# An encoder layer on one core: queries cast ahead of the fourth exponential, and the row tile, the norms and the residual additions in other places

## The chip, the cores and the metric

The kernel runs on one core of a Trainium2 chip. Its engines are TensorE (PE, whose weight loads are listed apart as PEld), VectorE (DVE), ScalarE (ACT), GpSimd (POOL) and SyncE (SP), which here only issues DMAs. Each engine works through its own instructions in order; semaphores hold an instruction until its inputs are there and its output's place is free. The metric is the time of one execution on the device, in microseconds. Before the change it was 1484.23 us, the median of three runs (1482.45 to 1485.06).

## The reference

One layer of a bidirectional encoder, applied to two sequences of 512 tokens with the same weights, all in float32:

```
def encoder_layer(x, ...):                       # x (1, 512, 1024)
    h = rms_norm(x, ln1)
    q, k, v, u, g_att, g_ssm = split(h @ w_in)   # 16 query heads and 4 key heads of 64
    q, k = rms_norm(q per head, q_gain), rms_norm(k per head, k_gain)
    y_att = windowed_attention(q, k, v, sink, bias, mask)   # blocks of 128, 3 key blocks each
    y_ssm = s5_branch(u, ...)                    # y * sigmoid(y @ w_glu + b_glu)
    mixed = sigmoid(g_att) * y_att + sigmoid(g_ssm) * y_ssm
    x = x + mixed @ w_out
    h2 = rms_norm(x, ln2)
    return x + square(relu(h2 @ w_up)) @ w_down  # 1024 -> 4096 -> 1024
```

## The kernel before

Both sequences go through the layer together, 1024 tokens, in tiles of 128 rows (partitions). Every large product is done in three matmuls: an operand in float32 is split into a rounded part `hi`, cast by ACT, and the rest `lo`, subtracted by DVE, and PE adds up hi·hi, hi·lo and lo·hi (L115 to L117, and with other names L724, L753, L1177). So in front of nearly every matmul stand an ACT cast and a DVE subtraction. The order of the instructions of an engine follows the order in which the program gives them, but a scheduler may move them within limits, and the tiles of a pool decide which bytes of memory a tile gets, and with it for whom it must wait.

**Attention** runs in eight steps, one for each pair of a sequence and a key head, each of four units (a block of 128 queries with its four heads). In a unit `cur` is the unit whose scores are being made and `prev` the unit before it, whose probabilities are turned and multiplied by the values. `cur.scores(h)` is PE (L1048, into a bank of PSUM called `sps`), `cur.largest(h)` is DVE (L1052: adds the bias and finds the maximum `nmx`), `cur.exp(h)` is ACT (L1058). `prev.turn(j)` transposes on PE (L1064), `prev.high(j)` casts on ACT (`ph`, L1068), `prev.low(j)` subtracts on DVE (L1073), `prev.value(j, s)` multiplies on PE (L1080). `rows` is the set of queries for a block that comes later: `norm` (L1012), `turn` (PE, L1018), `high` (the cast `qa` on ACT, L1023) and `low` (its rest on DVE, L1027). Between these stand the projections for later steps on PE (`project`, L724), whose weights are loaded by SP (L717), cast by ACT (`w_hi`, L718) and subtracted by DVE. In the last step the products of the state-space branch take that place (L1177, with the operand `act` from ACT L1162 and DVE L1170). At the end of a step `Divide` makes the reciprocals of the sums of the probabilities: it turns them (L1106), copies them into the tile `row` (L1108, 16x128), stores them by DMA (L1109), loads them again spread out as `fac` (L1114) and multiplies on POOL (L1119).

**The gated mix** follows (L1490 to L1528): products with w_glu on PE (L753) whose weights are split by ACT (`c_hi`, L736) and DVE (`c_lo`, L737), and on DVE the gates, the mix of both branches and the split of the mixed rows `at` (L1516 to L1528), which are then multiplied by w_out. The tile pool `ap` holds the attention's tiles, the pool `wyp` those of the scan and of weights.

**The output projection and the second norm** (L1330 to L1680): the tokens of the second sequence go in three passes, t = 1 to 3. In each, `old.norm()` is the DVE operation L1439 (its factor `rs` comes from POOL, L1434), `old.turn()` the transposes of the result on PE (L1447), and `old.old_rows(0, 1)` two subtractions on DVE of rows of the first sequence (L1462).

**The MLP** is done with seven products in place of eight (Strassen and Winograd): the four quarters of the operands are first added to or subtracted from each other. In the down projection `product_d(n)` (L1907) makes product n in groups of two row pairs r = 0, 2, 4 and so on: the piece of the left operand `d_a` and of the weights `k1`, `k2`, `k3` are loaded, combined on DVE (L1923), and both are split, with casts on ACT (L1928) and subtractions on DVE (`a_lo`, `b_lo`, L1929). Then come 24 matmuls into four banks. The results are added up in the tiles q1, q3, q4, q5 (128x2048 each), to which the residual `xq`, loaded from memory, is added by one DVE operation each: L1948 ahead of product 5, L1955 ahead of product 6 and L1970 ahead of product 2.

Of the kernel before, what the change touches and what calls it, by code (L numbers as in the profile page):

```python
# [11 lines left out]
F32 = mybir.dt.float32  # L12
# [6 lines left out]
P = 128  # L19
# [10 lines left out]
G = 4  # L30
HD = 64
BLOCK = 128
NB = SEQ // BLOCK
# [30 lines left out]
def hybrid_layer(ctx, tc, x, xT, rel, onehot, early, w_qkv, w_ug, q_gain, k_gain, sink,  # L64
                 b_re, b_im, c_re, c_im, d_skip, w_glu, b_glu, w_out, ln2, w_up, w_down, out):
    nc = tc.nc
    V, S, PE, GP, SP = nc.vector, nc.scalar, nc.tensor, nc.gpsimd, nc.sync
# [203 lines left out]
    with tc.tile_pool(name="xin", bufs=2, reuse_waits="tile") as xin, tc.tile_pool(name="ssmc", bufs=1) as sc:  # L271
# [10 lines left out]
        rows, columns, first_w = {}, {}, []  # L282
# [670 lines left out]
    with tc.tile_pool(name="att", bufs=2, reuse_waits="tile") as ap:  # L953
# [138 lines left out]
        class Divide:  # L1092
# [10 lines left out]
            def turn(self):  # L1103
                j, sq = self.j, self.sq
                pt = tps()
                PE.transpose(pt[0:G * NB, 0:P], self.rs, ident)  # L1106
                row = ap.tile([G * NB, P], F32, tag="row", name="row", bufs=1)
                S.copy(row, pt[0:G * NB, 0:P])  # L1108
                self.queue.dma_start(rs_scr[sq, j * G:(j + 1) * G, :].rearrange("h (b t) -> (h b) t", b=NB), row)  # L1109
                self.fac = (ap.tile([P, 2, HALF], F32, tag="ya", name="fac") if self.last  # L1110
                            else evp.tile([P, 2, HALF], F32, tag="ev", name="fac"))
                for e in range(2):
                    src = rs_scr[sq, j * G + e, :]
                    self.queue.dma_start(self.fac[e * 64:(e + 1) * 64],  # L1114
                                         bass.AP(rs_scr.tensor, src.offset, [[0, 64], [2 * HALF, 2], [1, HALF]]))
# [83 lines left out]
        if True:  # L1199
            rows = entry()  # L1200
            for i, (j, sq) in enumerate(steps):
# [8 lines left out]
                for qb in range(NB):  # L1210
# [72 lines left out]
                        div.turn()  # L1283
                    if n3:
                        prev.value(1, 0)
                    cur.exp(3)
                    if n3 > 2:
                        prev.low(2)
                    if rows:
                        rows.high()  # L1290
                        rows.low()
                    project(4)
                    if i == len(steps) - 1:
# [295 lines left out]
    with tc.tile_pool(name="wout", bufs=1, reuse_waits="tile") as wb:  # L1589
        w_last = [wb.tile([P, KT, HALF], F32R, name=f"w{i}_23") for i in range(2)]  # L1590
        w4 += [[q[:, k:k + 4, :] for q in w_last] for k in (0, 4)]
        rows0 += [Rows(0, t) for t in range(2, 4)]
        ln2_bc = rn2.tile([P, D], F32, name="ln2_bc", bufs=1)
        SP.dma_start(ln2_bc, ln2.to_broadcast([P, D]))

        def pieces(n):
            for _ in range(n):
                nxt = raws[-1][0] + 1
                split_piece()
                if nxt < 2 * KT:  # L1600
                    load_piece(nxt)

        for k in (0, 4):
            for t in range(2):
                rows0[t].part(0, k, k + 4)
                if k:
                    rows0[t].end(0)()
                    pieces(1)
        for t in range(2, 4):
            for k in (0, 4):  # L1610
                rows0[t].part(0, k, k + 4)
                if k:
                    rows0[t].end(0)()
                pieces(1)
        for t in range(2):
            rows0[t].part(1, 0, 4)
            pieces(1)
        for t in range(4):
            if t < 2:
                rows0[t].part(1, 4, KT)  # L1620
                rows0[t].end(1)()
            else:
                rows0[t].half(1)()
            if t:
                rows0[t - 1].norm()
            if t > 1:
                rows0[t - 2].turn()
                rows0[t - 2].first_rows()
        rows1 = [Rows(1, 0)]
        add = rows1[0].half(0)  # L1630
        rows0[2].turn()
        rows0[2].first_rows()
        rows0[3].norm()
        t4 = slot_b.tile([P, KT, HALF], F32R, tag="act0", name="t4")
        T4 = [t4[:, 0:4, :], t4[:, 4:8, :]]
        add()
        add = rows1[0].half(1)
        rows0[3].turn()
        rows0[3].first_rows()
        for t in range(1, 4):  # L1640
            old = rows1[t - 1]
            rows1.append(Rows(1, t))
            nxt_add = rows1[t].half(0)
            add()
            if t > 1:
                rows1[t - 2].sums_b()
                rows1[t - 2].sums_c()
            old.old_rows(0, 1)
            old.norm()
            old.turn()  # L1650
            add = rows1[t].half(1)
            if t == 3:
                raws0 = [wb0.tile([P, 4, P], F32, tag="w_raw", name="u_raw0", bufs=2) for _ in range(2)]
                for i, raw in enumerate(raws0):
                    SP.dma_start(raw, w_up[0, :, i])
                up_raws = {0: slot_b.tile([P, 4, 4, P], F32, tag="b0", name="u_raw"),
                           1: slot_b.tile([P, 4, 4, P], F32, tag="b1", name="u_raw")}
                for r, raw in up_raws.items():
                    for i in range(2):
                        SP.dma_start(raw[:, i * 2:i * 2 + 2], w_up[r, :, i * 2:i * 2 + 2])  # L1660
                homes = [wb0.tile([P, 4, 4, P], F32R, tag=f"w{i}", name=f"f_{i}") for i in range(2)]
            nxt_add()
            if t == 3:
                first = [[(homes[r][:, 2 * i], homes[r][:, 2 * i + 1]) for i in range(2)] for r in range(2)]
                for raw, home in zip(raws0, first[0]):
                    first_parts(raw, home)()
            old.sums_a()
# [125 lines left out]
    def bank():  # L1793
        return ps_m.tile([P, HALF], F32, tag="bank", name="bank")
# [103 lines left out]
    with tc.tile_pool(name="down0", bufs=2, side="right", reuse_waits="tile") as d0, \  # L1898
# [5 lines left out]
        k2, k3 = [[dc.tile([P, 2, HALF], F32, name=f"k{i}_{r}") for r in range(NPAIR // 2)] for i in (2, 3)]  # L1904
        q1, q3, q4, q5 = [dc.tile([P, 4, HALF], F32, name=f"q{i}") for i in (1, 3, 4, 5)]

        def product_d(n):  # L1907

            ps = entry_ps if n == 1 else [bank() for _ in range(4)]
            for r in range(0, NPAIR, 2):  # L1910
                rs = slice(r, r + 2)
# [13 lines left out]
                for src, tag in ((a, "a"), (b, "b")):  # L1925
                    hi = (d0 if tag == "a" else dp).tile([P, 2, HALF], F32R, tag=tag + "_hi", name=tag + "_hi")
                    lo = dp.tile([P, 2, HALF], F32R, tag=tag + "_lo", name=tag + "_lo")
                    S.copy(hi, src)  # L1928
                    V.tensor_sub(lo, src, hi.bitcast(F32))  # L1929
                    hl.append((hi, lo))  # L1930
                pair_products(ps, hl, r)
            return ps

# [5 lines left out]
        def store(src, t, sq, c):  # L1939
            row = sq * HALF + t * P  # L1940
            SP.dma_start(out[row:row + P, c * HALF:(c + 1) * HALF], src)

        ps = product_d(1)
        SP.dma_start(k1[0], w_down[0, 0, :, 0:2, :])
        for t in range(4):
            S.copy(q1[:, t], ps[t])
        xq = residual(0, 0)
        V.tensor_add(q3, q1, xq)  # L1948
        xq = residual(0, 1)
        ps = product_d(5)  # L1950
        for t in range(4):
            S.copy(q5[:, t], ps[t])
            V.tensor_add(q4[:, t], q5[:, t], xq[:, t])
        xq = residual(1, 1)
        V.tensor_add(q5, q5, xq)  # L1955
        ps = product_d(6)
        for t in range(4):
            V.tensor_add(q1[:, t], ps[t], q1[:, t])
            V.tensor_add(q4[:, t], q1[:, t], q4[:, t])
# [6 lines left out]
        for t in range(4):  # L1966
            V.tensor_add(q1[:, t], ps[t], q1[:, t])
            V.tensor_add(q5[:, t], q5[:, t], q1[:, t])
            store(q5[:, t], t, 1, 1)
        V.tensor_add(q1, q1, xq)  # L1970
        ps = product_d(2)
        for t in range(4):
            V.tensor_add(q3[:, t], ps[t], q3[:, t])
            store(q3[:, t], t, 0, 0)
# [78 lines left out]
```

## Time and profile before

| | |
|---|---|
| median of three runs | 1484.23 us |
| the profiled execution | 1483.69 us |
| its span, from the first to the last instruction | 1481.9 us |
| mean granted clock of PE | 0.997 |
| instructions | 21572 |
| DMA | 243.86 MB in 129238 packets |

The profile is that of one execution. In its rows the first number is the start in us from the begin of the span, the second the busy time in us, then engine, line, operation, output, inputs and shape; x2 says that the row stands for two such instructions in a run. In brackets stands how long the engine had been idle and what ended it. A row with SPq is the issue of a DMA on SP. In the list of waits a row says who waited for which tile, by whom it was released, and the waiting time in all, how many times, and the mean.

### The profile page before, as it was taken

The numbers are of one execution on the slowest core, as the hardware profiler recorded it, in microseconds if no ns is written. First come the engines' busy times: TensorE is split into PE (matmuls) and PEld (weight loads), VectorE is DVE, ScalarE is ACT, GpSimd is POOL, SyncE is SP. The second block draws the span as 40 slices with busy tenths as digits, with TensorE's granted clock in tenths as the row PEclk, the third lists the DMA queues.
The fourth block names the chain that finished last, engine by engine and source line by source line (L and its number), as shares of the span: only waits on it lengthen the run. The fifth ranks groups of instructions, "written<-read, shape, count | busy, mean of one in ns | idle before, by whom it ended". The sixth has DMA issues, their size and how long they took to land.

```text
span 1481.9 us, 21572 instructions
## 1 busy us (share of the span) xinstructions
PE 1454.6 (98%) x7782; PEld 1235.8 (83%) x7782; DVE 1093.8 (74%) x1827; ACT 764.2 (52%) x1366; POOL 168.2 (11%) x270
## 2 busy tenths in 40 slices
PE   7999999999999999999999999999999999999998
PEld 5888888888998888987788888888888878888787
DVE  7799979964636888888973688877776588575553
ACT  5589862224426777787432355555545443333332
POOL 4111120000312333343100000000000000000000
PEclk9999999999999999999999999999999999999999
DMA  8355567359841313236864135544443894454441
GB/s 301 107 174 176 166 208 252 119 177 290 282 121 51 106 51 87 88 129 200 285 221 147 71 113 172 167 146 156 157 156 121 300 340 148 156 175 152 128 128 58
DMA packets 129238, 243.86 MB, mean 165 GB/s; under 512 B 16059, under 2 KB 59323, under 8 KB 129132
## 3 DMA queue, kind: packets, MB, share of 16 engines
q1 hardware_dynamic: 104684, 186.87, 40.1%
q10 hardware_dynamic: 21888, 46.15, 8.3%
q0 software_dynamic: 2560, 9.48, 2.0%
q8 instruction: 61, 1.00, 0.3%
q14 instruction: 45, 0.37, 0.1%
HBM read 173.20 MB, written 81.82 MB: 172 GB/s over the span
## 4 chain that ended last, share of the span: by engine, by line
PE 87%; DVE 5%; issue 3%; ACT 2%; DMA 2%; POOL 1%; SPq 0%; DVEq 0%; ACTq 0%; POOLq 0%
PE bank L116 13%; PE bank L117 13%; PE bank L115 13%; PE acc L141 11%; PE acc L724 7%; PE acc L753 4%; PE acc L115 3%; PE acc L117 3%; PE acc L116 3%; PE sps L604 2%; PE po L1080 2%; PE sps L860 2%; PE sps L1048 2%; PE tps L1064 2%; PE lag L619 1%
## 5 line engine op out<-in xcount | busy, mean ns | idle before, releaser
L116 PE MATMUL bank<-b_lo,a_hi 128*128 128x512 f32 x440 | 171.4, 390 | 2.4 <-DVE b_lo L1929 2.4
L117 PE MATMUL bank<-b_hi,a_lo 128*128 128x512 f32 x440 | 171.2, 389 | 0.0
L115 PE MATMUL bank<-b_hi,a_hi 128*128 128x512 f32 x440 | 170.5, 389 | 0.0
L724 PE MATMUL acc<-w_hi,hT 128*128 128x256 f32 x768 | 165.0, 292 | 0.0
L141 PE MATMUL acc<-hT,c_hi 128*128 128x512 f32 x512 | 161.1, 394 | 0.0
L1928 ACT CAST a_hi<-d_a 128x1024 fp32r<-128x1024 f32 x55 | 57.8, 1051 | 181.5 <-PE bank L116 178.5
L1929 DVE TENSOR_TENSOR a_lo<-d_a,a_hi 128x1024 fp32r<-128x1024 f32 x55 | 67.4, 1225 | 102.0 <-ACT a_hi L1928 99.9
L724 PEld LDWEIGHTS acc<-w_hi,hT 128*128 128x128 f32 x768 | 126.7, 190 | 1.7
L141 PEld LDWEIGHTS acc<-hT,c_hi 128*128 128x128 f32 x512 | 94.6, 188 | 21.1 <-issue 2.5
L724 PE MATMUL acc<-w_lo,hT 128*128 128x256 f32 x384 | 108.2, 282 | 0.0
L141 PE MATMUL acc<-hT,c_lo 128*128 128x512 f32 x256 | 100.2, 392 | 0.0
L117 PE MATMUL bank<-act,u_lo 128*128 128x512 f32 x256 | 99.6, 389 | 0.0
L115 PE MATMUL bank<-act,u_hi 128*128 128x512 f32 x256 | 99.6, 389 | 0.0
L116 PE MATMUL bank<-act,u_hi 128*128 128x512 f32 x256 | 99.6, 389 | 0.0
L116 PEld LDWEIGHTS bank<-b_lo,a_hi 128*128 128x128 f32 x440 | 82.6, 188 | 20.3 <-DVE b_lo L1929 3.2
L115 PEld LDWEIGHTS bank<-b_hi,a_hi 128*128 128x128 f32 x440 | 82.6, 188 | 17.3
L117 PEld LDWEIGHTS bank<-b_hi,a_lo 128*128 128x128 f32 x440 | 82.6, 188 | 17.1
L1058 ACT ACTIVATE p<-p,nmx 128x257 f32<-128x257 f32 (+1 forms) x128 | 72.2, 564 | 35.4 <-DVE nmx L1052 34.8
L724 PEld LDWEIGHTS acc<-w_lo,hT 128*128 128x128 f32 x384 | 73.0, 190 | 2.5
L1052 DVE CUSTOM_DVE_ANT_0 p<-sps,bias,nsink 128x256 f32<-128x256 f32 (+1 forms) x128 | 69.3, 542 | 2.9 <-PE sps L1048 0.4
L1713 ACT CAST u_hi<-s 128x512 fp32r<-128x512 f32 x64 | 39.3, 621 | 59.8 <-PE bank L116 36.9
L1929 DVE TENSOR_TENSOR b_lo<-k,b_hi 128x1024 fp32r<-128x1024 f32 x55 | 67.1, 1220 | 0.0
(389 smaller groups left out, 3627.8 us busy)
## 6 DMA issues: line engine op xcount, KB each, us to landing
d_a<-a_scr SPq DMA_DIRECT2D x55, 512.0 KB, 3.6
u_raw<-in_w_up_dram SPq DMA_DIRECT2D x32, 512.0 KB, 5.9
a_scr<-t ACTq DMA_DIRECT2D x64, 256.0 KB, 2.1
k<-in_w_down_dram SPq DMA_DIRECT2D x32, 512.0 KB, 5.7
a_scr<-a ACTq DMA_DIRECT2D x48, 256.0 KB, 3.3
c_raw<-in_w_ug_dram SPq DMA_DIRECT2D x44, 256.0 KB, 3.5
ct_scr<-ctab SPq DMA_DIRECT2D x16, 576.0 KB, 3.3
ctab_in<-ct_scr SPq DMA_DIRECT2D x32, 288.0 KB, 4.9
```

Of the source, the lines that this page charges most:

```text
L115: PE.matmul(ps, a[0], b[0], start=first, stop=False)
L116: PE.matmul(ps, a[0], b[1], start=False, stop=False)
L117: PE.matmul(ps, a[1], b[0], start=False, stop=last)
L141: PE.matmul(self.ps[s], self.w[p == 2][:, k, :], hT[s][p == 1][:, k, :], start=i % (3 * KT) == 0, stop=i % (3 * KT) == 3 * KT - 1)
L604: PE.matmul(ps[:, i * P:(i + 1) * P], bm[:, ri, g, :], u_sb[:, g, :], start=True, stop=True)
L724: PE.matmul(ps, act[p == 2][:, k, col:col + P], self.w[k // 4][p == 1][:, k % 4, :], start=i == 0, stop=i == 3 * KT - 1)
L753: PE.matmul(self.ps[s], w_g[self.m][p == 2][:, k, :], y_part(s, int(p == 1), k), start=k + p == 0, stop=k == KT - 1 and p == 2)
L1052: V.tensor_tensor_reduce(self.p[:, h, 1:1 + self.nk], self.s[h][:, 0:self.nk], biases[self.j][h][:, b0:b0 + self.nk], -1.0, nsink[:, hh:hh ...
L1058: S.activation(p, p, AF.Exp, bias=self.nmx[:, h:h + 1], scale=-1.0, accum_out=self.sums[:, h, self.qb:self.qb + 1])
L1713: S.copy(hi, src)
L1928: S.copy(hi, src)
L1929: V.tensor_sub(lo, src, hi.bitcast(F32))
```

## The change

It has four parts.

1. In the units whose `prev` has two key blocks and in which no keys are copied, the cast of the queries (`rows.high()`) is given ahead of `cur.exp(3)` instead of behind it. There is one such unit in each of the eight steps.
2. The tile `row` comes from the pool `wyp` instead of `ap`.
3. `old.norm()` is given ahead of `old.old_rows(0, 1)`.
4. Three of the additions of `xq` (128x2048) are made in four parts of 128x512 each and handed to `product_d`, which gives one of them in each group from the second on.

```
-                row = ap.tile([G * NB, P], F32, tag="row", name="row", bufs=1)
+                row = wyp.tile([G * NB, P], F32, tag="row", name="row", bufs=1)
...
+                    sooner = rows and n3 == 2 and not kd
+                    if sooner:
+                        rows.high()
                     cur.exp(3)
                     if n3 > 2:
                         prev.low(2)
                     if rows:
-                        rows.high()
+                        if not sooner:
+                            rows.high()
                         rows.low()
...
+            old.norm()
             old.old_rows(0, 1)
-            old.norm()
             old.turn()
...
-        def product_d(n):
-
+        def product_d(n, aside=()):
+
+            aside = list(aside)
...
+                if r and aside:
+                    aside.pop(0)()
                 pair_products(ps, hl, r)
...
+        def added(dst, src, xq):
+            return [lambda t=t: V.tensor_add(dst[:, t], src[:, t], xq[:, t]) for t in range(4)]
...
-        V.tensor_add(q3, q1, xq)
+        ps = product_d(5, added(q3, q1, xq))
         xq = residual(0, 1)
-        ps = product_d(5)
...
-        V.tensor_add(q5, q5, xq)
-        ps = product_d(6)
+        ps = product_d(6, added(q5, q5, xq))
...
-        V.tensor_add(q1, q1, xq)
-        ps = product_d(2)
+        ps = product_d(2, added(q1, q1, xq))
```

On ACT, in the unit of step 1 that makes the scores of its second block, the order is now the following (the difference; L1058 are exponentials, L1108 the copy into `row`, L1023 the cast of the queries, L1001 the squares for the norm of the next ones, L1084 a copy of the values' result):

```order
 L1058 ACTIVATE p,sm<-p,nmx 128x385
 L1108 COPY row<-tps 16x128
-L1058 ACTIVATE p,sm<-p,nmx 128x385
-L1023 ACTIVATE qa<-acc,gain_q 128x4x128
+L1023 ACTIVATE qa<-acc,gain_q 128x4x128
+L1058 ACTIVATE p,sm<-p,nmx 128x385
 L1001 ACTIVATE sq<-acc 128x256
 L1084 COPY ol<-po 64x512
```

The cast has changed places with the fourth exponential, and nothing else has moved there; on DVE `rows.low()` stands where it stood.

On SP, at the same place of step 1 (L717 are loads of weights for the projections, L1109 is the store of `row`, L1214 a copy within memory for the scan):

```order
 L717 DMA w_raw_5242<-in_w_qkv_dram 128x512
 L1214 DMA y2_scr_84<-y_scr_83 16x64x128
+L1109 DMA rs_scr_93<-row_5328 16x128
 L717 DMA w_raw_5349<-in_w_qkv_dram 128x512
-L1109 DMA rs_scr_93<-row_5328 16x128
 L717 DMA w_raw_5680<-in_w_qkv_dram 128x512
 L1214 DMA y2_scr_84<-y_scr_83 16x64x128
```

The store of `row` has moved ahead of one load of weights.

On DVE, at the start of product 5 in the down projection, the order before was (L1923 combines pieces of weights, L1929 splits, L1948 is the addition of the residual):

```order
L1929 TENSOR_TENSOR b_lo_12612<-k1_0_12316,b_hi_12611 128x1024
L1923 TENSOR_TENSOR k2_0_12324<-k3_0_12332,k2_0_12324 128x1024
L1923 TENSOR_TENSOR k1_0_12316<-k3_0_12332,k1_0_12316 128x1024
L1923 TENSOR_TENSOR k2_1_12325<-k3_1_12333,k2_1_12325 128x1024
L1929 TENSOR_TENSOR a_lo_12644<-d_a_12639,a_hi_12643 128x1024
L1948 TENSOR_TENSOR q3_12341<-q1_12340,xq_12594 128x2048
L1929 TENSOR_TENSOR b_lo_12648<-k1_1_12317,b_hi_12647 128x1024
L1923 TENSOR_TENSOR k2_2_12326<-k3_2_12334,k2_2_12326 128x1024
```

and it is now (the lines L1923, L1929 and L1948 of before are L1928, L1934 and L1951 here):

```order
L1934 TENSOR_TENSOR b_lo_12609<-k1_0_12316,b_hi_12608 128x1024
L1928 TENSOR_TENSOR k2_0_12324<-k3_0_12332,k2_0_12324 128x1024
L1951 TENSOR_TENSOR q3_12341<-q1_12340,xq_12594 128x512 x3
L1928 TENSOR_TENSOR k1_0_12316<-k3_0_12332,k1_0_12316 128x1024
L1934 TENSOR_TENSOR a_lo_12641<-d_a_12636,a_hi_12640 128x1024
L1934 TENSOR_TENSOR b_lo_12645<-k1_1_12317,b_hi_12644 128x1024
L1951 TENSOR_TENSOR q3_12341<-q1_12340,xq_12594 128x512
L1928 TENSOR_TENSOR k1_1_12317<-k3_1_12333,k1_1_12317 128x1024
L1928 TENSOR_TENSOR k2_1_12325<-k3_1_12333,k2_1_12325 128x1024
```

Three of the four quarters stand ahead of the second `b_lo`, the fourth behind it, and one combination of weights (`k2_1`) has moved behind it as well.

## The prediction

> **What bounds the kernel.** I read the page first, then what TensorE (PE) waited for, then each of those places in order of time.
>
> ```profile
> PE 1454.6 (98%) x7782; PEld 1235.8 (83%) x7782; DVE 1093.8 (74%) x1827; ACT 764.2 (52%) x1366; POOL 168.2 (11%) x270
> PE 87%; DVE 5%; issue 3%; ACT 2%; DMA 2%; POOL 1%; SPq 0%; DVEq 0%; ACTq 0%; POOLq 0%
> ```
> PE works 1454.6 of the 1481.9 us of the span, and the chain of work that ended last runs on PE for 87% of it. No other engine is near its limit, so only two things make this kernel shorter: fewer or shorter matmuls, or fewer waits of PE. The change leaves PE's instructions as they are (their order differs in two groups of matmuls only). What it can gain lies within the 27 us in which PE does nothing, and the four kinds of wait that its parts aim at are these (waiting us, times, mean us):
>
> ```profile
> PE sps L1048 <- DVE nmx L1052: 3.3, 7, 0.5
> PE bank L116 <- DVE b_lo L1929: 2.4, 2, 1.2
> PE acc L753 <- DVE c_lo L737: 2.0, 1, 2.0
> PE tps L1447 <- DVE rn_xn L1439: 0.8, 2, 0.4
> ```
> Together 8.5 us, with 12 waits. A wait costs more than its idle time, since the matmul behind it starts in an empty pipeline: below I take the loss from start to start, against the spacing of the same matmuls elsewhere.
>
> **Queries ahead of the fourth exponential.** Step 1, between the blocks 1 and 2 (us from the span's start, busy us, then idle before):
>
> ```profile
> 494.14 0.62 ACT L1058 ACTIVATE p<-p,nmx 128x385 f32<-128x385 f32 x1 [0.74 <-DVE nmx L1052]
> 494.76 0.67 ACT L1023 ACTIVATE qa<-acc,gain_q 128x512 fp32r<-128x512 f32 x1
> 494.90 0.60 PE L1064 MATMUL tps<-ident,p 128*128 128x128 f32 x4
> 495.46 0.76 DVE L1027 SCALAR_TENSOR_TENSOR qa<-acc,gain_q,qa 64x512 fp32r<-64x512 f32 x1 [1.35 <-ACT qa L1023]
> ...
> 495.93 0.40 PE L724 MATMUL acc<-w_hi,hT 128*128 128x256 f32 x2
> 496.17 0.28 PE L724 MATMUL acc<-w_lo,hT 128*128 128x256 f32 x1
> 496.25 0.62 DVE L1052 CUSTOM_DVE_ANT_0 p<-sps,bias,nsink 128x384 f32<-128x384 f32 x1
> ...
> 496.93 0.44 PE L1048 MATMUL sps<-kh,qa 128*128 128x384 f32 x1 [0.48 <-DVE nmx L1052]
> ```
> PE's score product of block 2 (496.93) needs a bank of PSUM that DVE reads last in `largest` (496.25). That stands behind `rows.low` (495.46), which waited 1.35 us for ACT's cast of the queries `qa` (494.76), and the cast stood behind exponential 3 (494.14), ahead of which ACT had been idle 0.74 us. PE's matmuls follow each other at 0.12 there (two from 495.93 to 496.17); from 496.17 to 496.93 it is 0.76, so 0.64 is lost. After the change the cast (0.67) runs within ACT's idle 0.74, and exponential 3 starts at 494.14 as before, since it waits for DVE's `nmx` anyway. `low` starts at about 494.1, `largest` at 494.9 and ends at 495.5, before PE comes to that product at 496.29 (496.93 less 0.64). The stall goes. The cover is thin: were exponential 3 late, PE's `turn` at 494.90, right behind its end at 494.76, would be late by as much.
>
> Of the seven waits in the list one stands between blocks 0 and 1, where the keys' copies keep the old order. Six are of the kind shown, one of them in step 1, which has a bill of its own (next). Five times 0.64: **3.2**.
>
> In step 1 SP's order changes too: the store of the row tile now stands ahead of a weight load that stood ahead of it.
>
> ```profile
> 493.42 0.33 SPq L1109 DMA_DIRECT2D rs_scr<-row  x1
> ...
> DMA to landing us min/median/max: 3.1/3.5/4.2
> ...
> 496.21 0.62 ACT L718 CAST w_hi<-w_raw 128x512 fp32r<-128x512 f32 x1
> 496.85 0.59 ACT L1068 CAST ph<-tps 128x512 fp32r<-128x512 f32 x1
> ...
> 498.30 0.39 PE L1080 MATMUL po<-ph,va 128*128 128x512 f32 x1
> ```
> The store can't be issued before the row is copied, 493.42; the load behind it is issued 0.33 later, at 493.75, and lands 3.1 to 4.2 us after that (the weight pieces' landings in this stretch): 496.9 to 498.0. ACT's cast `w_hi` of that piece, due at 496.21 − 0.64 = 495.6, waits for it and holds `ph` (0.59) behind itself, which is ready 0.62 + 0.59 after the landing: 498.1 to 499.2. PE's `value`, which reads `ph`, stood at 498.30. So step 1 gains 0.2 at best and loses 0.9 at worst, and I take −0.5, nearer to the worst, since the median landing is 3.5 and ACT has other work queued there.
>
> Step 7 moves block 0 alone:
>
> ```profile
> 664.24 0.76 DVE L1027 SCALAR_TENSOR_TENSOR qa<-acc,gain_q,qa 64x512 fp32r<-64x512 f32 x1 [1.25 <-ACT qa L1023]
> 665.06 0.48 PE L1177 MATMUL acc<-act,c_hi 128*128 128x512 f32 x1
> ...
> 665.75 0.50 PE L1177 MATMUL acc<-act,c_hi 128*128 128x512 f32 x1 [0.22 <-DVE act L1170]
> ```
> There `low` waited 1.25 us for `qa`, and behind it on DVE stands the product `act`, for which PE waited. Start to start 0.69, where 128x512 matmuls stand 0.23 apart (1219.04, below, has two in 0.61, the last of 0.39): **0.46** that goes, as ACT had the exponential ahead of the cast here too. Queries in all 3.2 − 0.5 + 0.46 = 3.2, bounds 0 and 4.3 (all six and step 7).
>
> **The row tile.** In the gated mix, where PE waits longest (the row of a window gives the busy time of PE, PEld, DVE, ACT and POOL, then PE's granted clock and the DMAs' share):
>
> ```profile
> 703.17 0.69 DVE L1528 TENSOR_TENSOR act<-at,act 128x512 fp32r<-128x512 f32 x1 [3.23 <-DMA rs_scr<-row]
> 707.34 0.69 DVE L1516 TENSOR_TENSOR at<-z,at 128x512 f32<-128x512 f32 x1
> 710.39 2.37 POOL L1119 TENSOR_TENSOR ya<-ya,fac 128x1024 f32<-128x1024 f32 x1 [5.55 <-DMA fac<-rs_scr]
> 710.51 2.79 DVE L1516 TENSOR_TENSOR at<-z,at 128x512 f32<-128x512 f32 x1
> 713.23 1.28 DVE L737 TENSOR_TENSOR c_lo<-c_raw,c_hi 128x512 fp32r<-128x512 f32 x2
> ...
> 713.97 0.50 PE L753 MATMUL acc<-act,c_lo 128*128 128x512 f32 x1 [2.02 <-DVE c_lo L737]
> ...
> 714.00:720.00 6.00, 6.00 (x19) 4.76 (x20) 5.29 (x7) 2.21 (x4) 0.00 (x0) 0.72 0.96 312
> ...
> 725.62 1.28 DVE L737 TENSOR_TENSOR c_lo<-c_raw,c_hi 128x512 fp32r<-128x512 f32 x2
> 726.62 0.39 PE L753 MATMUL acc<-act,c_lo 128*128 128x512 f32 x1
> ```
> DVE's second cast of the mix (703.17) waits 3.23 us for the DMA that stores the last `row`: its target lies in the bytes of that tile. Everything behind it on DVE is late by that much, up to `c_lo` (713.23), for which PE waits 2.02 us. With 0.17 of start-up behind it PE loses 2.19. Right after it the granted clock is 0.72 in the stretch 714 to 720; 6 us at 0.72 are worth 4.3 at full clock, that is, 1.7 us more is lost (the stretches beside it have 1.00). With `row` in another pool the wait goes; DVE's op can then start when ACT's part of the cast is done, about 700.1, that is 3.07 earlier. Its old place in memory is free long before, and the new one lies under the first piece of w_out, which is written some 25 us later.
>
> What is late next? DVE is busy 5.29 of 6.00 us in 714 to 720, so it is itself the bound there: it is 3.07 ahead at most. Without the wait and the slow clock PE would be 2.19 + 1.7 = 3.9 ahead. The next pair of `c_lo` (725.62, first one done at 726.3) serves PE at 726.62 with a reserve of 0.32. So PE may gain 3.07 + 0.32 = **3.4**, and waits for the other 0.5 in the next column. Bounds: 0 if the wait is handed on whole (rival B), 3.9 if DVE has reserves that I don't see.
>
> One row there is no gain: DVE's 710.51 takes 2.79 where the same operation takes 0.69 at 707.34, and it ends 0.5 us after POOL's product of 2.37 that began 0.12 ahead of it. POOL's product waits for its own DMA, so after the change it will meet some other instruction of DVE's chain, and the 2.1 stay; I credit nothing. The Trainium skill, SBUF — State Buffer, section "Who interferes with whom", says that a DVE instruction with two SBUF inputs contends with a GpSimd instruction that reads SBUF and that the loser is blocked fully; the trace agrees, with 2.79 against 0.69. On the clock the Trainium skill, TensorE: Matmul & The Clock Gate, section "What's actually happening", has a free-running window of about 3.4 us that must be idle before the clock halves; by that rule a wait of 2.02 would not be the cause, and the slow stretch would stay. The trace has it right behind this wait and nowhere else in this stage; by the skill's rule the row tile brings 2.2 instead of 3.4, which rival B prices.
>
> **The norm ahead of the old rows.**
>
> ```profile
> 841.91 0.57 POOL L1434 TENSOR_TENSOR rs<-rs,neg_half 128x1 f32<-128x1 f32 x1
> ...
> 843.08 1.29 DVE L1462 TENSOR_TENSOR s<-act,act 128x512 f32<-128x512 f32 x2
> 844.29 1.28 DVE L1439 SCALAR_TENSOR_TENSOR rn_xn<-x,rs,ln_bc 128x1024 f32<-128x1024 f32 x1
> ...
> 844.90 0.39 PE L117 MATMUL acc<-w,act 128*128 128x512 f32 x1
> ...
> 845.71 0.63 PE L1447 MATMUL tps<-ident,rn_xn 128*128 128x128 f32 x4 [0.42 <-DVE rn_xn L1439]
> ```
> `rs`, which the norm needs, is ready at 842.48, but DVE does the two subtractions of the old rows first (843.08, 1.21 from start to start), then the norm (844.29). PE's transposes start 0.8 after the matmul before them (844.90), which at 0.23 apart would be 845.13: 0.58 lost. In the new order the norm ends at 844.4, 0.7 early. The subtractions end when the norm did, and DVE's sum of work is the same. The waits' list has it twice, so 2 × 0.58 = 1.16, of which I take **1.1**. The first of the three passes has no such wait to lose. There the subtractions now come 1.21 later, behind a norm that waits for `rs`, and DVE has idle time behind them: a loss between 0 and 1.2, taken as 0, since PE shows no wait for them.
>
> **Residual additions in quarters.** In the down projection:
>
> ```profile
> 1217.39 2.29 DVE L1948 TENSOR_TENSOR q<-q,xq 128x2048 f32<-128x2048 f32 x1
> 1219.04 0.61 PE L115 MATMUL bank<-b_hi,a_hi 128*128 128x512 f32 x2
> 1219.59 1.22 DVE L1929 TENSOR_TENSOR b_lo<-k,b_hi 128x1024 fp32r<-128x1024 f32 x1
> ...
> 1220.86 0.50 PE L116 MATMUL bank<-b_lo,a_hi 128*128 128x512 f32 x1 [1.21 <-DVE b_lo L1929]
> ```
> The addition of 128x2048 (2.29; 2.20 to the next start) stands ahead of `b_lo` (1219.59), for which PE waits: the product at 1220.86 was due at 1219.49 (two of 0.23 from 1219.04), 1.37 lost. In the new order three quarters stand ahead of it and the subtraction for a later piece stands behind it. A quarter's shape takes 0.69 (707.34) by itself and a fourth of 2.20 is 0.55; at 0.60 each, and 1.13 for that subtraction (the shape of `b_lo`, 1.22, less the same overlap of 0.09): 1219.59 − 2.20 − 1.13 + 1.80 = 1218.06, and `b_lo` is done at 1219.28. PE comes to it at 1219.27 in the new order, in which one product and not two stands ahead of it. The list has this wait twice; the other is in product 2, 2.4 − 1.21 = 1.2 and the same 0.16 of start-up, 1.35. The third addition, ahead of product 6, is in no wait, and its quarters bring nothing. 2.7 less 0.1 for the quarters that now stand in later groups: **2.6**, bounds 0 (all of it handed on, rival C) and 2.7.
>
> **Sum.** 3.2 + 3.4 + 1.1 + 2.6 = 10.3. The profiled execution took 1483.69 (span 1481.9), and the median of three runs is 1484.23, so it stands for them: 1483.7 − 10.3 = **1473.4**.
>
> **Rivals.**
> A. *The queries bring nothing.* The cast overruns ACT's idle time, exponential 3 is late, and PE waits at `turn` instead of at the score product. For it: 0.07 us to spare, and `turn` follows exponential 3 within 0.14. Against it: the cast's inputs are there before the idle time begins, and exponential 3 waits for `nmx` in any case. 1473.4 + 3.2 = 1476.6.
> B. *The wait for the row is handed on.* The products behind L1528 on DVE need tiles that DMAs bring, and POOL's 2.37 may meet a worse instruction, so `c_lo` comes no earlier: 1473.4 + 3.4 = 1476.8. For it: the DMAs are busy 0.96 of 714 to 720. Against it: no instruction of DVE behind 703.17 up to `c_lo` shows a wait for a DMA. A part of it: PE's clock dips without the long wait, so that only the 2.19 is won, 1474.6.
> C. *The quarters fill DVE.* A later `b_lo` of products 5 and 2 comes late in the place of this one, for the same instructions stand on the same engine. For it: the 0.01 by which the first is late already. Against it: two waits in the whole list, so the groups behind had room. 1473.4 + 2.6 = 1476.0.
> D. *The change doesn't show:* every wait is replaced by another of its size on the same engine, 1483.
> E. *Slower.* The weight load of step 1: SP issues in order, so whatever holds the row's store holds this load, ACT's queue behind `w_hi`, and PE. Its price is the landing's time less 497: from a landing at 510.3 on it takes back the 10.3 and 3 more, 1486.7 or above. For it stands the order alone; the row of landings (4.2 at most after the issue) speaks against 16.
>
> **How the numbers follow.** Forecast 0.58, A 0.14, B 0.14 (0.05 of it for the clock), C 0.07, D 0.04, E 0.03. A measurement of this kernel can tell about 0.2%, 3 us, from no change. Forecast, A, B and C lie more than that below 1483.7: faster 0.93; D is same, 0.04; E slower, 0.03. The best bounds of the terms are 4.3 + 3.9 + 1.16 + 2.7 = 12.0, that is 1471.7, and the fastest run of before is 1.2 below the profiled one: low end 1470.5. At the other end stands B's 1476.8, and the slowest run is 1.4 above the profiled one: 1478.2. Outside are D, E and two of A, B and C at once.
>
> **What would show it.** Queries: the waits PE sps on DVE nmx fall from 7 to 1 or 2, and `qa` stands ahead of the exponential in ACT's idle time. Step 1: `w_hi` waits for a DMA at about 496, `value` is late by about 1. Row: DVE's L1528 starts at 700 and the idle before `c_lo`'s matmul and the clock of 0.72 are gone; wrong, if a DVE wait on another DMA or POOL's product stands there. Norm: no wait of the transposes on `rn_xn`. Quarters: no wait of PE bank on `b_lo` above 0.3; wrong, if there are more and shorter ones. The prediction as a whole is wrong if PE has fewer waits and its matmuls are longer.

## The result and the profile after

The changed kernel takes 1470.84 us (median of five runs, 1469.22 to 1472.85) against 1483.62 before; the ratio is 0.991 with a 95% interval of 0.9897 to 0.9924, that is 11.3 to 15.3 us less. The forecast was 10.3 us less and its range ended at 1470.5; the ratio puts the time at 1470.3. Measured once more on another occasion the median was 1468.26 against 1482.93. So the direction was right, and the forecast gain was too small by 2.5 to 4. The profiled execution took 1469.22 (span 1467.4) and is the fastest of the five.

The page's row on busy times, and the list of PE's waits (the numbers of such a row are the us in all, how many times, and the longest of them, not the mean), where the rows for `c_lo` and for `b_lo` are gone:

```profile
PE 1446.3 (99%) x7782; PEld 1234.1 (84%) x7782; DVE 1094.6 (75%) x1836; ACT 764.2 (52%) x1366; POOL 168.9 (12%) x270
...
PE po L1080 <- ACT ph L1068: 1.2, 2, 0.6
...
PE sps L1048 <- DVE nmx L1052: 0.5, 1, 0.5
...
PE tps L1451 <- DVE rn_xn L1443: 0.2, 1, 0.2
```

The seven waits for `nmx` are down to one, as forecast. But PE's busy time fell too, from 1454.6 to 1446.3, with the same 7782 instructions: 8.3 us of the 14.5 by which the span is shorter were never booked as idle (about 1.6 of it is the slow clock in the gated mix). The two traces have the same matmuls in the same order, apart from the two groups in the down projection, so the start of each can be set against its start before. This table is worked out from those starts (us against the profiled execution of before, from the span's start; minus is earlier); the other four columns are the experiments below:

```
time in before      after   only_queries  only_row  only_norm  only_quarters
455  attention      +1.0        +0.1        -0.1      +0.1        -0.1
700  its end        -6.7        -7.1         0.0      +0.1        -0.1
724  gated mix     -10.7        -9.0        -4.0      -2.2        -2.2
760  its end       -10.7        -6.3        -3.7      -1.3        +0.1
890  after norms   -11.5        -6.4        -3.7      -2.1         0.0
1230 product 5     -13.1        -7.6        -5.1      -3.2        -1.5
1475 end           -14.5        -7.6        -5.1      -3.2        -3.0
```

Between 455 and 700 the changed kernel gains 7.7 us, where the prediction had 3.2. The gated mix gives 4.0 (3.4 forecast), the norms 0.8 (1.1), the down projection 3.0 (2.6). Of the +1.0 at 455, 0.8 is a matmul of the scan, ahead of the attention, that waited for ACT and came late; no part of the change touches it.

Where do the other 4.5 us of the attention come from? The prediction read PE's list of waits, in which `pl` (DVE's rest of the probabilities) has two. PE's weight loads, listed apart as PEld, have their own list; before, then after (455 to 700):

```profile
PEld po L1080 <- DVE pl L1073: 8.6, 30, 0.5
PEld sps L1048 <- DVE nmx L1052: 6.3, 14, 0.7
```
```profile
PEld po L1080 <- DVE pl L1073: 3.9, 12, 0.5
...
PEld sps L1048 <- DVE nmx L1052: 2.1, 7, 0.7
```

Thirty weight loads waited for `pl` before, twelve do now. One of the eighteen that are gone, in step 2, 2.4 us behind the wait that the prediction took away (before, then after):

```profile
528.66 0.34 PE L1048 MATMUL sps<-kl,qa 128*128 128x384 f32 x1
528.98 0.19 PEld L1080 LDWEIGHTS po<-pl,va 128*128 128x128 f32 x1 [0.30 <-DVE pl L1073]
528.98 0.50 PE L1080 MATMUL po<-pl,va 128*128 128x512 f32 x1
```
```profile
527.69 0.34 PE L1048 MATMUL sps<-kl,qa 128*128 128x384 f32 x1
527.86 0.39 PE L1080 MATMUL po<-pl,va 128*128 128x512 f32 x1
```

The weight load stood 0.30 us for `pl`, and the matmul started 0.32 after the one before it instead of 0.17. PE shows no idle time there, since the matmul before is still recorded as busy when the next one should have started; what shows is a busy time of 0.50 instead of 0.39. Such a place costs 0.15 at its start and 0.11 in its start-up, both booked as busy.

Step 1, whose loss had been forecast, is as described. The rows of SP, ACT and PE after:

```profile
493.14 0.33 SPq L1109 DMA_DIRECT2D rs_scr<-row  x1
493.58 0.83 SPq L717 DMA_DIRECT2D w_raw<-in_w_qkv_dram  x2
...
496.74 0.62 ACT L718 CAST w_hi<-w_raw 128x512 fp32r<-128x512 f32 x1 [1.30 <-DMA w_raw<-in_w_qkv_dram]
...
498.02 0.51 PE L1080 MATMUL po<-ph,va 128*128 128x512 f32 x1 [0.61 <-ACT ph L1068]
```

The weight load is issued at 493.58, behind the store of the row, `w_hi` waits 1.30 us for it, and `value` is 0.76 late (the new one of the two waits for `ph` in the list). The stall ahead of it that went was worth 0.82, so step 1 comes out at about nothing.

In the gated mix (DVE, POOL, and a window with PE's granted clock and the DMAs' share behind the busy times):

```profile
693.38 0.69 DVE L1532 TENSOR_TENSOR act<-at,act 128x512 fp32r<-128x512 f32 x1 [0.16 <-ACT act L1531]
...
705.02 2.73 POOL L1119 TENSOR_TENSOR ya<-ya,fac 128x1024 f32<-128x1024 f32 x1 [7.30 <-DMA fac<-rs_scr]
705.53 3.23 DVE L1518 TENSOR_TENSOR z<-gl,gs 128x512 f32<-128x512 f32 x1
...
704.00:710.00 6.00, 6.00 (x28) 4.99 (x27) 5.93 (x5) 1.17 (x2) 3.51 (x2) 1.00 1.02 386
```

DVE no longer waits for the row's store. POOL's product has moved on to another victim, as expected: `z` takes 3.23 where it takes 1.15 elsewhere. PE works through, at full clock. At the last norm there is a new wait, which nobody had forecast:

```profile
857.00 1.28 DVE L1443 SCALAR_TENSOR_TENSOR rn_xn<-x,rs,ln_bc 128x1024 f32<-128x1024 f32 x1
...
858.42 0.63 PE L1451 MATMUL tps<-ident,rn_xn 128*128 128x128 f32 x4 [0.18 <-DVE rn_xn L1443]
```

### The profile page after: what moved, and what is told of

It reads as the page before. It is cut to its first block, busy times and chain, and to the rows that moved or that the text cites. A ratio compares the mean times of both kernels' runs of the same rounds, so it can differ in the third digit from the quotient of the medians.

```text
span 1467.4 us, 21580 instructions
## 1 busy us (share of the span) xinstructions
PE 1446.3 (99%) x7782; PEld 1234.1 (84%) x7782; DVE 1094.6 (75%) x1836; ACT 764.2 (52%) x1366; POOL 168.9 (12%) x270
## 4 chain that ended last, share of the span: by engine, by line
PE 91%; DVE 3%; ACT 2%; DMA 1%; issue 1%; POOL 1%; SPq 0%; DVEq 0%; ACTq 0%; POOLq 0%
PE bank L115 14%; PE bank L116 14%; PE bank L117 14%; PE acc L141 11%; PE acc L724 8%; PE acc L753 5%; PE acc L115 3%; PE acc L117 3%; PE acc L116 3%; PE po L1080 2%; PE sps L604 2%; PE sps L1048 2%; PE sps L860 2%; PE tps L1064 2%; PE lag L619 1%
## 5 line engine op out<-in xcount | busy, mean ns | idle before, releaser
L1934 DVE TENSOR_TENSOR a_lo<-d_a,a_hi 128x1024 fp32r<-128x1024 f32 x55 | 67.3, 1223 | 99.4 <-ACT a_hi L1933 97.3
L1058 ACT ACTIVATE p<-p,nmx 128x257 f32<-128x257 f32 (+1 forms) x128 | 72.1, 564 | 27.0 <-DVE nmx L1052 24.3
L1934 DVE TENSOR_TENSOR b_lo<-k,b_hi 128x1024 fp32r<-128x1024 f32 x55 | 66.9, 1217 | 0.0
```

The lines of the kernel that those rows point to most:

```text
L1058: S.activation(p, p, AF.Exp, bias=self.nmx[:, h:h + 1], scale=-1.0, accum_out=self.sums[:, h, self.qb:self.qb + 1])
```

## The experiments

The first four do one part of the change each, on the kernel before. Theory 1: a late instruction of DVE makes PE restart several times, in places that PE's list of waits doesn't name, so the cast alone gives the whole gain of the attention. Theory 2, the rival: the cast wins its listed waits only, and other parts, such as the place of the row tile, gave the rest.

**only_queries**

```
+                    sooner = rows and n3 == 2 and not kd
+                    if sooner:
+                        rows.high()
                     cur.exp(3)
```

> Only the cast of the queries is moved; row tile, norms and residual additions as before. Theory 1 (many small restarts: behind each late DVE instruction follow two or three more waits of PE, of 0.1 to 0.3 us, that show only as longer distances between matmuls): PE is 7.2 to 8.2 us earlier at the end of the attention (about 700) against before, 1.2 to 1.3 per step in steps 0, 2, 3, 4 and 6, about 0 in step 1, and the kernel takes about 1476. Theory 2 (the cast wins its six listed waits only, and the rest of the gain in the attention comes from the other parts, the place of the row tile above all): 3.2 us at 700, 1480.4 in all. The wait of 2.0 us for c_lo stays under both.

Measured: 1475.59 against 1483.29, ratio 0.9942 (0.9929 to 0.9956). Its PE is 7.1 us earlier at 700, with 1.3 per step in steps 3, 4 and 6. Theory 1 holds, theory 2 is out. The order of SP in step 1 is that of the changed kernel, so that swap belongs to the cast, not to the row tile. Two rows of its list of waits, and the window behind one of the waits for `c_lo`:

```profile
PE acc L753 <- DVE c_lo L737: 4.1, 2, 2.4
...
PE bank L116 <- DVE b_lo L1933: 1.2, 1, 1.2
...
720.00:726.00 6.00, 5.86 (x26) 4.86 (x27) 5.97 (x9) 3.62 (x7) 0.00 (x0) 1.00 0.91 288
```

Here the parts that were not changed behave otherwise than in the trace of before: PE waits twice for `c_lo`, 4.1 us in all instead of 2.0, with the clock at 1.00 behind it (PEclk is the third number from the end), and only once for `b_lo` instead of twice. No part of the change touches either, so what one execution shows of them is one outcome among several; this matters for the next points.

**only_row**

```
-                row = ap.tile([G * NB, P], F32, tag="row", name="row", bufs=1)
+                row = wyp.tile([G * NB, P], F32, tag="row", name="row", bufs=1)
```

> Only the row tile is in the other pool. Theory 1: nothing happens ahead of 700; from 700 to 724 PE gains 3.6 to 4.0 us, of which 2.0 to 2.4 is the wait for c_lo and 1.5 the slow clock behind it; about 1479.9. Theory 2: besides this some 4 us in the attention, 1476. A third theory (the clock's slow stretch is not caused by the wait): the gain from 700 to 724 is 2.2 and a slow stretch of about 3.4 us is still in the trace.

Measured: 1478.61 against 1483.29, ratio 0.9968 (0.9956 to 0.9981). Nothing changes ahead of 700; from 700 to 724 PE gains 4.0, and 0.3 comes back in the next column. That is theory 1. No instruction of any engine stands elsewhere than before, so this is the wait alone. In the list of waits the seven for `nmx` are unchanged, and in product 5, DVE's combination of weights has no wait ahead of it:

```profile
PE sps L1048 <- DVE nmx L1052: 3.3, 7, 0.5
...
PE bank L116 <- DVE b_lo L1929: 1.2, 1, 1.2
```
```profile
1207.78 3.50 DVE L1923 TENSOR_TENSOR k<-k,k 128x1024 f32<-128x1024 f32 x3
...
1214.53 1.22 DVE L1929 TENSOR_TENSOR b_lo<-k,b_hi 128x1024 fp32r<-128x1024 f32 x1
```

In the profiled execution of before the same three instructions had waited 1.26 us for a DMA that brings the weights, and this made `b_lo` late:

```profile
1212.84 3.50 DVE L1923 TENSOR_TENSOR k<-k,k 128x1024 f32<-128x1024 f32 x3 [1.26 <-DMA k<-in_w_down_dram]
```

Without it PE loses 0.03 at that place, in only_queries 0.18 and in only_norm 0.34, against 1.37. So about half of what the prediction credited to the quarters was one late DMA of one execution.

**only_norm**

```
+            old.norm()
             old.old_rows(0, 1)
-            old.norm()
```

> Only the norms are ahead of the old rows. If the wait of 0.3 us at the last norm, which is new after the change, is made by this part alone (PE is early and DVE's chain up to the last norm is not): PE gains 0.57 twice and gives 0.3 to 0.5 back at about 870, 0.7 in all. If it comes from the other parts: 1.1 and no wait there. 1482.6 to 1483.1.

Measured: 1482.15 against 1483.29, ratio 0.9993 (0.9984 to 1.0002), too small for the timing alone. The trace is clear: 0.63 and 0.62 won at the second and third pass, 0.5 given back at the last norm and the product ahead of it, 0.7 in all. The new wait is made by this part alone:

```profile
PE tps L1447 <- DVE rn_xn L1439: 0.2, 1, 0.2
```

The last norm's inputs pass through ACT, POOL and DVE one after the other, and this chain gained less than PE did.

**only_quarters**

The four edits of the down projection from the diff above, and nothing else.

> Only the residual additions are in quarters. Both waits of PE for b_lo go with nothing in their place: 1.5 and 1.4, 2.9 us in all, about 1480.8. If later groups take over the wait (DVE has no reserve): less than 1.5 in all, with waits for other b_lo of products 5 and 2 in the list.

Measured: 1480.79 against 1483.29, ratio 0.9981 (0.9972 to 0.9989); in the trace 1.5 and 1.4, and no wait for `b_lo` is left, so no later group took one over. By the three executions above the first of the two is worth between 0 and 1.4 and the second, in product 2, 1.3 each time. That makes 1.3 to 2.7, and the ratio has 1.6 to 4.2; how often the weights come late in the kernel before, one profile of it can't tell.

**no_row**: the changed kernel with the row tile back in `ap`.

> The changed kernel with the row tile back in its old pool; the order of all engines is that of the changed kernel. If the parts add up: the wait for the row's store is back (2.6 to 3.2 us on DVE), PE loses 2.2 to 4.4 us from 700 to 760 and nothing elsewhere, 1473 to 1475.2. If the row's place also helped the attention (theory 2): PE is some 4 us later at 700 than in the changed kernel.

Measured: 1472.39, ratio to the kernel before 0.9941 (0.9927 to 0.9955). Against the trace of the changed kernel PE has the same gain from 455 to 700 and loses 2.9 from 700 to 760, by two waits for `c_lo`:

```profile
PE acc L753 <- DVE c_lo L737: 2.3, 2, 1.6
```

In the traces the parts add up; the time is 0.6 below the range that was expected. In the five executions with the old place PE lost 2.2, 4.4, 2.2, 3.8 and 2.6 us to `c_lo`.

**dve_late**: the changed kernel, with DVE held up again at the place where it used to wait for the cast, while ACT keeps its new order. The reductions add work whose result isn't used.

```
                         elif qb == 1:
                             for _ in range({0: 6, 2: 6, 3: 3, 4: 3}.get(i, 0)):
                                 V.reduce_sum(late, ident.rearrange("p (a b) -> p a b", a=G), axis=AX.X)
                         rows.low()
```

> The changed kernel with small reductions on DVE (128 elements, 0.2 to 0.3 us each; their result isn't used) ahead of rows.low in block 1: six in steps 0 and 2, three in steps 3 and 4, none in step 6. ACT's order stays that of the change. Theory 1a (a backlog on DVE makes all the restarts): steps 0 and 2 give back nearly all of their 1.3 us, also at the later places (value and scores of the two units behind), steps 3 and 4 a part, step 6 nothing. Theory 1b (the later restarts come from ACT, where the cast no longer stands ahead of the casts of the probabilities): steps 0 and 2 give back at most the 0.75 of the first wait, and the later places keep the distances of the changed kernel.

Measured: 1472.81 (one run). The steps with six reductions lost 1.8 each, those with three 0.8 each, step 6 nothing. Step 2, DVE, then PE and its weight load:

```profile
523.48 1.90 DVE L1298 TENSOR_REDUCE late<-ident 128x4 f32<-128x128 f32 x6
...
525.40 0.76 DVE L1027 SCALAR_TENSOR_TENSOR qa<-acc,gain_q,qa 64x512 fp32r<-64x512 f32 x1
...
526.87 0.45 PE L1048 MATMUL sps<-kh,qa 128*128 128x384 f32 x1 [0.98 <-DVE nmx L1052]
...
528.90 0.33 PE L1048 MATMUL sps<-kl,qa 128*128 128x384 f32 x1
529.21 0.19 PEld L1080 LDWEIGHTS po<-pl,va 128*128 128x128 f32 x1 [0.30 <-DVE pl L1073]
529.22 0.51 PE L1080 MATMUL po<-pl,va 128*128 128x512 f32 x1
```

The 1.90 us make the first wait longer than it was before (0.98 against 0.48), and the later places come back to what they were: the weight load waits 0.30 for `pl`, and the distance is 0.32, as before, instead of 0.17. The other three restarts of the step have before's distances to 0.01 as well (0.34, 0.33 and 0.31), and the weight loads of the attention that wait for `pl` are 24, against 12 without the reductions. So theory 1a holds: the restarts come from DVE's backlog, not from ACT's order. One thing moved that was not meant to: on SP the store of `row` in step 1 stands behind the weight load again, as before the change. `value` isn't late there, and step 1, which has no reductions, gains 0.9 on the changed kernel; so the time of this run tells less than its trace.

**store_pool**: the changed kernel, but the row of step 1 is stored from GpSimd's queue.

```
-                self.queue.dma_start(rs_scr[sq, j * G:(j + 1) * G, :]...
+                queue = GP if (j, sq) == (0, 0) else self.queue
+                queue.dma_start(rs_scr[sq, j * G:(j + 1) * G, :]...
```

> The changed kernel, but the row tile of step 1 is stored from GpSimd's queue, so that SP's weight load does not stand behind it. If SP's order makes step 1's loss: value in step 1 is not late, and PE gains 0.7 to 0.8 us more in step 1 and nothing elsewhere. If ACT is held by something else there: no change.

Measured: 1469.91 (one run). `value` is not late, and step 1 gains 0.87: SP's order was its loss. Ten us later PE waited for something else, because POOL's product of that step came late: the store that its factors wait for landed 4.5 us after its issue:

```profile
501.95 2.39 POOL L1120 TENSOR_TENSOR ya<-ya,fac 128x1024 f32<-128x1024 f32 x1 [4.52 <-DMA fac<-rs_scr]
...
506.95 0.66 PE L1018 MATMUL acc<-ident,qn 128*128 128x128 f32 x4 [1.45 <-POOL qn L1013]
```

In the next kernel, with the same store, it landed after 2.5 us, the product starts at 499.95 and PE has no such wait.

**two_pool**: as store_pool, and the cast stands ahead of the fourth exponential in block 0 too.

```
-                    sooner = rows and n3 == 2 and not kd
+                    sooner = rows and n3 == 2
```

> As the run before, and the cast of the queries stands ahead of the fourth exponential in block 0 of steps 0 to 6 too, where the keys are copied. If DVE's backlog is the cause there as well: 0.3 to 0.5 us for each of seven steps, with step 1's 0.75 some 3 to 4 us, about 1467. If ACT has no idle time there, because it also casts the keys: exponential 3 is late, turn waits in its place, and there is no gain beyond the 0.75.

Measured: 1465.91, ratio to the kernel before 0.9888 (0.9874 to 0.9901). From 455 to 700 its trace gains 3.0 us on that of the changed kernel: 0.9 in step 1 and about 0.3 in each unit with the new order. Its list of weight loads that wait:

```profile
PEld po L1080 <- DVE pl L1073: 3.3, 10, 0.5
...
PEld sps L1048 <- DVE nmx L1052: 0.7, 1, 0.7
```

**sooner_two**: this edit without the store on GpSimd.

> The changed kernel with the cast ahead in block 0 of steps 0 to 6 too, the row's store on SP as in the changed kernel. If the gains of that and of the store on GpSimd are separate: 3.0 of the 3.9 us by which two_pool was ahead, with step 1's 0.75 to 0.85 still lost: 1468.

Measured: 1467.37 (one run). From 455 to 700 it gains 1.0 on the changed kernel, less than expected. Against two_pool it loses 0.68 at step 1's `value`, as expected, but also 0.6 behind it, where PE waits for POOL's `qn` as in store_pool, and 0.4 in step 7. So the two edits don't simply add: whether POOL's product of step 1 gets in the way depends on when its DMA lands.

**all_pool**: `sooner = rows`, in all units.

> As two_pool, and the cast ahead of the fourth exponential in all units, also those with three key blocks in which ACT was idle 0.56 us and the cast takes 0.67. DVE's wait there was 0.75. If DVE's backlog counts there too: 0 to 2 us below two_pool's 1465.9. If exponential 3 comes late and turn waits for it: 0 to 2 us above.

Measured: 1463.95, ratio to the kernel before 0.9873 (0.9858 to 0.9887), the fastest of all. From 455 to 700 its trace gains 2.1 us on two_pool's: 0.2 in a unit with three key blocks in most steps, where the restarts at `pl` go, and the rest in the first blocks of steps 0 and 1. Once, at 457, `turn` starts 0.26 late, for an exponential that comes late behind the cast, which is the forecast's rival A in small.

**after_again**: the changed kernel a second time.

> The changed kernel once more, beside the run of the other two. If its gain is the sum of the parts as the traces have it (queries 7 to 7.7, row 2.2 to 4.4, norms 0.7, quarters 1.4 to 2.9): 1469.5 to 1472, and no wait of PE in products 5 and 2.

Measured: 1468.26 against 1482.93, ratio 0.9901 (0.9884 to 0.9917). But the gated mix of its profiled execution (DVE, PE, and the window behind) shows that the stall of the row tile isn't gone for good:

```profile
710.91 1.23 DVE L1508 TENSOR_TENSOR gs<-gs,yr 128x1024 f32<-128x1024 f32 x1 [1.03 <-ACT c_hi L736]
...
713.46 0.69 DVE L1393 TENSOR_TENSOR w<-w_raw,w 128x512 fp32r<-128x512 f32 x1 [1.31 <-DMA mix_scr<-ya]
...
716.52 0.80 PE L753 MATMUL acc<-act,c_lo 128*128 128x512 f32 x1 [2.14 <-DVE c_lo L737]
...
717.00:720.00 3.00, 3.00 (x8) 2.35 (x8) 2.97 (x5) 0.66 (x3) 0.00 (x0) 0.51 0.76 244
```

DVE waited 1.03 us, by the profile for ACT, and then 1.31 us for the store of POOL's product, the next link of the same chain of DMAs. That store landed 6.6 us after its issue, where the trace of the first run of this kernel has 4.3. PE waited 2.14 us for `c_lo`, with the clock at 0.51 behind it: 4.05 us in all.

Why did the clock fall here and in the trace of before, and not in only_queries, where PE waited longer for `c_lo`? In both the stretch of half clock is 3.41 us long. Here are that stretch and the one of the same length ahead of it, in before and in after_again; then, for only_queries, the two stretches that share its wait of 2.36 us, counted on in steps of 3.41 us from the start of the trace's record of the clock (PE's busy time is the second number):

```profile
712.08:715.49 3.41, 1.52 (x7) 1.25 (x8) 3.41 (x4) 2.15 (x3) 1.46 (x2) 1.00 0.68 232
715.49:718.90 3.41, 3.41 (x10) 2.63 (x9) 3.34 (x5) 0.01 (x1) 0.00 (x0) 0.50 0.99 341
...
713.13:716.54 3.41, 1.27 (x7) 0.73 (x5) 3.05 (x5) 0.64 (x2) 0.00 (x0) 1.00 0.54 183
716.54:719.96 3.42, 3.42 (x8) 2.77 (x9) 3.39 (x5) 1.08 (x2) 0.00 (x0) 0.50 0.75 252
...
715.42:718.83 3.41, 2.36 (x11) 1.63 (x9) 3.38 (x6) 0.22 (x1) 0.00 (x0) 1.00 0.68 198
718.83:722.25 3.42, 2.10 (x9) 1.77 (x10) 3.42 (x5) 1.21 (x2) 0.00 (x0) 1.00 0.93 278
```

The two shorter waits lay within one stretch, but for 0.1 us, and these stretches had 1.52 and 1.27 us of work; the longer one was cut in two, and no stretch had less than 2.10. These rows fit a clock that follows the work done in each such stretch. Where its limit lies, they leave open: 1.86 us of work in only_quarters were followed by 1.00, 1.88 at the start of store_pool by 0.50.

## Why the prediction was wrong, point by point

- *"What it can gain lies within the 27 us in which PE does nothing."* This step failed. The gain is smaller than 27 us, but it doesn't lie there: 8.3 us of it were booked as busy. About 1.6 of these are the slow clock, which the term of the row tile did count; most of the others had no term.
- *"Five times 0.64: 3.2."* This term was mis-sized, and it made the sum too small. The mechanism and the place were right. Each of these steps gave 1.3: 0.75 at the named wait with its start-up, and about 0.55 at three or four places behind it, where PE waited for `pl` or `nmx` on the same late DVE. Step 5 gave 0.5 where nothing was credited, step 7 0.8 instead of 0.46, and step 1 about nothing instead of −0.5. In all 7.7 (7.1 in only_queries) for 3.2. The prediction's own rule, that a wait costs more than its idle time, was applied to the listed waits, and not to those that the list leaves out.
- *The row tile, 3.4.* Right in mechanism: the DMA wait went, POOL's hold moved to another DVE instruction, and the new place cost nothing. The size hangs on the execution. With the old place PE lost 2.2 to 4.4 to `c_lo` (mean 3.0 of five), with the new one mostly 0 to 1.1, and 2.3 once (mean 0.5 of eight): 2.5 in the mean. The reserve of 0.32 at the next `c_lo`, on which the sum rested, was not a constant but one outcome of the DMAs. Rival B, the wait handed on to the next DMA, happened in after_again.
- *The clock.* The prediction credited up to 1.7 for a slow stretch behind the wait, and about 1.6 went. Behind waits for `c_lo` of 2.0 and 2.1 us it came (before, after_again); behind 1.7 and 2.4 us (only_queries) and 2.0 us (only_quarters) it stayed away. The Trainium skill, TensorE: Matmul & The Clock Gate, section "What's actually happening", has the clock halve after an idle window of about 3.4 us that runs free of the kernel. The runs agree that the place of the wait counts; they differ in that PE needn't be idle all that time: 1.9 and 2.1 us of 3.41 were enough.
- *The norms, 1.1.* Two waits of 0.57 went as said. 0.4 to 0.5 came back at the last norm, which the prediction had not looked at: 0.7. (The two DVE operations that changed places with the norm are additions, not subtractions; their price is the same.)
- *The quarters, 2.6.* 3.0 in the pair of traces, and `b_lo` came in time. But 1.0 to 1.3 of it stood on a DMA that was late in the one profiled execution; in the other three traces with the old additions the two places cost 1.3 to 1.7.
- *Rivals A, C, D and E* did not occur in the changed kernel: exponential 3 still waits for `nmx` behind the cast, no later group waits for `b_lo`, and the late load of step 1 cost 0.76.

Put together from the traces: 7.1 to 7.7, 2.5, 0.7 and about 1.5 make 11.8 to 12.4, beside a measured 12.8 with 11.3 to 15.3. So it is partly luck that the forecast missed by no more than 2.5 to 4: the attention was credited 4.5 too little, and the other three terms together some 2 too much. How the whole divides is less certain than the whole. The times of the four kernels with one part each give 7.7, 4.7, 1.1 and 2.5, 16.0 in all, against 12.8 and 14.7 in the two measurements of the whole; the intervals are wide enough for that. Whether slow clock behind waits for `c_lo`, or the late weights, come in more executions of before than of the others was not tested.

## What to carry to other kernels

When an engine is late ahead of a nearly full PE, count all matmuls behind it that start later than their usual distance, not the waits that PE's list names: weight loads that wait, and matmuls whose busy time is longer than that of their kind, show the rest. Before a term is credited whole, ask whether the wait hangs on a DMA, since then one profile has one draw of it. And where a cast feeds a second engine, put it in the idle time ahead of a stage that has to wait anyway; here this was worth more with every unit in which it was done.

## What had not been expected of the hardware

- A wait of PE's weight load of 0.3 us leaves no idle time in PE's rows: the matmul behind it is booked 0.50 instead of 0.39, and its start is 0.15 late.
- The clock fell to 0.72 and 0.51 (means of windows of 6 and 3 us) behind waits of 2.0 and 2.1 us, and stayed at 1.00 behind waits of 1.7, 2.0 and 2.4 us. Each time it was at 0.50 for 3.41 us, behind as long a stretch with 1.52 and 1.27 us of work.
- Where POOL's product and a DVE operation with two inputs in SBUF met, the latter ended 0.5 to 1.0 us behind POOL's end, as if it had started only then: 2.79 us for one of 0.69, 3.23 for one of 1.15. The Trainium skill, SBUF — State Buffer, section "Who interferes with whom", gives the rule that whoever issues first holds the shared ports for the whole instruction; these rows agree.
